# Three 256-column products in place of a 512- and a 256-column one, with the activations moved to another place in SBUF

## Chip, core and metric

The kernel runs on one core of a Trainium2 chip. The metric is the device time of one execution in microseconds, the median over runs. The profile is of one execution.

## What is computed

One decoder layer for 256 tokens of width 2048, in float32:

```python
h   = rmsnorm(x, attn_norm_g)
z   = h @ w_in                       # pool | q | k | v | indexer columns
x1  = x + concat(pool_mixer(...), dsa_attention(...)) @ w_out      # 2048 x 2048
up  = rmsnorm(x1, ffn_norm_g) @ w_up                               # 2048 x 11264
c   = conv_b + sum(conv_w[j] * shifted(up, j) for j in range(3))
gate, val = split(c, 2)
out = x1 + (silu(gate) * val) @ w_down                             # 5632 x 2048
```

## The kernel before

Every float32 operand of a large product is split into a high and a low half of type float32r, and a product is made of three terms: high x high, high x low and low x high. The activations stand as pairs (high, low) of 256 tokens each in three tiles: `xhl` (16 feature tiles; normed input first, then, overwritten, the input of the FFN), `yhl` (16, the input of w_out) and `ghl` (44, the input of w_down). The weights stream from HBM: `Unit.load` (L89) brings 1 MB into `raw` (two buffers), `Piece.split` (L103, L104) makes `whi` on ScalarE and `wlo` on VectorE (1024 columns each, four buffers of each), two pieces ahead of TensorE.

The order of the work is written out by hand: a list of pieces, each with its products, and `at(step, ...)`, which puts the other work between them. The stages run in this order: w_in in chunks (with the indexer, top-k, attention and pooling between them), w_out, w_up, w_down. For w_out, w_up and w_down the weight block of 128 x 128 is the stationary operand and the activations of 256 tokens move. One weight block (its high and its low half) with one feature tile is called a block here. There are 16 x 16 = 256 blocks in w_out, 88 x 16 = 1408 in w_up, and 16 x 44 = 704 in w_down.

A block is done by one of two helpers. `mm_feat` (L216, L217) loads the high weights once and streams both halves of the activations as one product of 512 columns, then loads the low weights and streams 256 columns. The products with the high and with the low half of the activations land in two halves of a PSUM bank, and whoever reads the result adds them (`up_out` L635 and L636, `down_out` L660 and L661). `mm_feat1` (L221 to L223) makes three products of 256 columns into one place, each with a weight load of its own. w_up and the first 14 of 16 column tiles of w_down use `mm_feat` (1408 + 616 blocks); w_out, the last two column tiles of w_down (88 blocks), the pool chunks of w_in and the pool mixer use `mm_feat1`. The other chunks of w_in (`mm_tok`, L210 to L212) hold the activations and move the weights, in products of 320 to 512 columns.

Where the tiles lie follows from the order of allocation, with no care for it in the code: modulo 512 bytes the weights' halves begin at 0, and one weight block is 512 bytes long in a partition; `xhl` begins at 256, `yhl` at 128, `ghl` at 0. The high or low half of a feature tile is 1024 bytes long, so all of a tile's halves begin at the same place modulo 512.

Of the kernel before, what the change touches and what calls it, by code (L numbers as in the profile page):

```python
# [8 lines left out]
F32 = mybir.dt.float32  # L9
F32R = mybir.dt.float32r  # L10
BF16 = mybir.dt.bfloat16
AF = mybir.ActivationFunctionType
ALU = mybir.AluOpType
AX = mybir.AxisListType

P = 128
S = 256
D = 2048
KT = D // P
IH = 16  # L20
DFF = 5632
NF = DFF // P
# [7 lines left out]
C_AG, C_FG, C_PS, C_QG, C_KG, C_IC, C_CW, C_CB = 0, 16, 32, 40, 41, 42, 58, 58 + 3 * 2 * NF  # L30
# [9 lines left out]
WARM = 8  # L40


@with_exitstack
def hybrid_kernel(ctx, tc, xT, par, wIa, wIb, wIc, wI2, wA, wU, wP, wO, wUp, wDn, out):
    nc = tc.nc
    PS = bass.MemoryType.PSUM

    cp = ctx.enter_context(tc.tile_pool(name="cp", bufs=1))
# [3 lines left out]

    pr = cp.tile([P, C_N], F32, name="pr")
    xf = cp.tile([P, KT, S], F32, name="xf")
    xhl = cp.tile([P, KT, 2, S], F32R, name="xhl")
    ga = cp.tile([P, KT], F32, name="ga")


# [32 lines left out]
    class Piece:  # L91


        def __init__(self, unit, a, b, mm):
            self.unit, self.a, self.b, self.mm = unit, a, b, mm
# [18 lines left out]
        sides.setdefault(step, []).append(lambda: f(*a))  # L114


    def split_x(k, src, gains, on_act):
        g = gains[:, k:k + 1]
        if on_act:
            nc.scalar.activation(xhl[:, k, 0], src, AF.Copy, scale=g)  # L120
        else:
            nc.vector.tensor_scalar(xhl[:, k, 0], src, g, None, op0=ALU.mult)
        nc.vector.scalar_tensor_tensor(xhl[:, k, 1], src, g, xhl[:, k, 0].bitcast(F32),  # L123
                                       op0=ALU.mult, op1=ALU.subtract)

    zp = ctx.enter_context(ExitStack())
    zc = zp.enter_context(tc.tile_pool(name="zc", bufs=1))
# [42 lines left out]
    r1, r2 = TokenNorm("r1"), TokenNorm("r2")  # L170
# [42 lines left out]

    def mm_feat(o, wh, wl, rhs, first, last):

        nc.tensor.matmul(o, wh, rhs.rearrange("p a t -> p (a t)"), start=first, stop=False)  # L216
        nc.tensor.matmul(o[:, 0:S], wl, rhs[:, 0], start=False, stop=last)  # L217

    def mm_feat1(o, wh, wl, rhs, first, last):

        nc.tensor.matmul(o[:, 0:S], wh, rhs[:, 0], start=first, stop=False)  # L221
        nc.tensor.matmul(o[:, 0:S], wh, rhs[:, 1], start=False, stop=False)  # L222
        nc.tensor.matmul(o[:, 0:S], wl, rhs[:, 0], start=False, stop=last)  # L223
# [13 lines left out]
    def pool_chunk(n):  # L237
        acc = Acc()
        for j in range(2):
            u = Unit(wU[2 * n + j], D)  # L240
            for h in range(2):
                def mm(p, j=j, h=h):
                    pt = acc.get()
                    for i in range(8):
                        k = 8 * h + i
                        mm_feat1(pt[:, j], *p.get(i * P, P), xhl[:, k], k == 0, k == KT - 1)
                pieces.append(Piece(u, h * 1024, (h + 1) * 1024, mm))
        return acc

    ia, za, ua, first = [], {}, [], {}  # L250
# [17 lines left out]
    for name in ORDER:  # L268
# [9 lines left out]
        else:  # L278
            c = ("k0", "k1", "q0", "q1", "v0", "v1").index(name)
            za[name] = tok_chunk([wA[c, q] for q in range(4)], 512)  # L280


    yhl = zc.tile([P, KT, 2, S], F32R, name="yhl")
    oa = [Acc() for g in range(8)]
    O0 = len(pieces)
    late = []
# [1 line left out]
    def mm_o(jp, j, ks, p, base):  # L288
        pt = oa[jp].get()
        for k in ks:  # L290
            mm_feat1(pt[:, j], *p.get((k - base) * P, P), yhl[:, k], k == 0, k == KT - 1)

    for jp in range(8):
        us = [Unit(wO[2 * jp + j], D) for j in range(2)]
        seq = [(j, h) for j in range(2) for h in range(2)]
        if jp == 0:
            seq = [(0, 0), (1, 0), (0, 1), (1, 1)]
        for j, h in seq:
            def mm(p, jp=jp, j=j, h=h):
                if jp == 0 and h == 1:  # L300
                    mm_o(jp, j, range(8, 14), p, 8)
                    late.append((jp, j, range(14, 16), p, 8))
                    if j == 1:
                        for a in late:
                            mm_o(*a)
                else:
                    mm_o(jp, j, range(8 * h, 8 * h + 8), p, 8 * h)
            pieces.append(Piece(us[j], h * 1024, (h + 1) * 1024, mm))
# [3 lines left out]
    for f in range(NF):  # L312
        us = [Unit(wUp[2 * f + j], D) for j in range(2)]
        seq = [(j, h) for j in range(2) for h in range(2)]
        if f == 0:
            seq = [(0, 0), (1, 0), (0, 1), (1, 1)]
        for j, h in seq:
            def mm(p, f=f, j=j, h=h):
                pt = ga_[f].get()
                for i in range(8):  # L320
                    k = 8 * h + i
                    mm_feat(pt[:, j], *p.get(i * P, P), xhl[:, k], k == 0, k == KT - 1)
            pieces.append(Piece(us[j], h * 1024, (h + 1) * 1024, mm))

    da = [Acc() for g in range(7)] + [Acc(single=True) for g in range(2)]
    D0 = len(pieces)
    ghl = None
    for i in range(16 * NF // 8):
        if i % 2 == 0:
            u = Unit(wDn[i // 2], 2048)  # L330

        def mm(p, i=i):
            for n in range(8):
                t, k = divmod(8 * i + n, NF)
                if t < 14:
                    mm_feat(da[t // 2].get()[:, t % 2], *p.get(n * P, P), ghl[:, k], k == 0, k == NF - 1)
                else:
                    mm_feat1(da[t - 7].get(), *p.get(n * P, P), ghl[:, k], k == 0, k == NF - 1)
        o = (i % 2) * 1024
        pieces.append(Piece(u, o, o + 1024, mm))  # L340

# [193 lines left out]
    pw_ = {}  # L535
# [49 lines left out]
    def pool_mix(n):  # L585
        g = GROUPS[n]
        hi, lo = pwt[n]
        for j in range(2):
            pt = ps_s.tile([P, 512], F32, name="pm", tag="ss")
            for k in range(2):  # L590
                c = slice(k * S + j * P, k * S + j * P + P)
                mm_feat1(pt, hi[:, c], lo[:, c], pw_[n][:, k], k == 0, k == 1)
            sc = pr[:, C_PS + 2 * g + j:C_PS + 2 * g + j + 1]
            y = yhl[:, 4 + 2 * n + 4 * (n == 3) + j]
            nc.scalar.activation(y[:, 0], pt[:, 0:S], AF.Copy, scale=sc)
            nc.vector.scalar_tensor_tensor(y[:, 1], pt[:, 0:S], sc, y[:, 0].bitcast(F32),
                                           op0=ALU.mult, op1=ALU.subtract)
# [4 lines left out]
    def x1_out(jp):  # L602
        pt = oa[jp].get()
        x1 = xf[:, 2 * jp:2 * jp + 2]
        nc.vector.tensor_tensor(x1, pt[:, :, 0:S], x1, op=ALU.add)
        for j in range(2):
            split_x(2 * jp + j, x1[:, j], pr[:, C_FG:C_FG + KT], True)
        if jp == 0:
            nc.scalar.activation(sq1, x1, AF.Square)
        else:  # L610
            t = zc.tile([P, 2, S], F32, name="xt", tag="t2", bufs=5)
            nc.scalar.activation(t, x1, AF.Square)
            nc.vector.tensor_tensor(sq1, sq1, t, op=ALU.add)
# [5 lines left out]
    fw = {}  # L619

    def ffn_open():
        nonlocal ghl
        zp.close()
        fp = ctx.enter_context(tc.tile_pool(name="fp", bufs=1))
        ghl = fp.tile([P, NF, 2, S], F32R, name="ghl")
        fw["up"] = [fp.tile([P, 2, S + 2], F32, name=f"up{i}") for i in range(2)]
        for u in fw["up"]:
            nc.gpsimd.memset(u[:, :, 0:2], 0.0)
        fw["fp"] = fp

    def up_out(f):
        fp = fw["fp"]
        pt = ga_[f].get()
        t = fp.tile([P, 2, S], F32, name="ft", tag="ft", bufs=2)
        nc.scalar.activation(t, pt[:, :, S:2 * S], AF.Copy)  # L635
        nc.vector.tensor_tensor(t, pt[:, :, 0:S], t, op=ALU.add)  # L636
        nc.vector.tensor_tensor(fw["up"][f % 2][:, :, 2:], t, r2.b2(), op=ALU.mult)

    def up_conv(f):
        u = fw["up"][f % 2]  # L640
# [16 lines left out]
    def down_out(jp):  # L657
        pt = da[jp].get()
        t = fw["fp"].tile([P, 2, S], F32, name="ft", tag="ft", bufs=2)
        nc.scalar.activation(t, pt[:, :, S:2 * S], AF.Copy)  # L660
        nc.vector.tensor_tensor(t, pt[:, :, 0:S], t, op=ALU.add)  # L661
        nc.vector.tensor_tensor(t, t, xf[:, 2 * jp:2 * jp + 2], op=ALU.add)
        nc.scalar.dma_start(out[:, 2 * jp:2 * jp + 2], t)

    def down_out1(jp, j):
# [80 lines left out]
    def prep(n):  # L746
        if n < 15 and n % 2 == 1:
            for k in (n + 1, n + 2):
                split_x(k, xf[:, k], ga, True)
        if n < len(pieces):  # L750
            pieces[n].split(2 if n == 0 else 1)
        if n == 0:
            for k in range(2):
                split_x(k, xf[:, k], ga, False)
# [73 lines left out]
```

## Time and profile before

| | us |
|---|---|
| median of 3 runs (lowest, highest) | 1098.84 (1098.68, 1098.87) |
| the profiled execution: its own time | 1098.5 |
| the profiled execution: span from first to last instruction | 1096.8 |
| TensorE busy in the span | 1090.8 |
| VectorE busy | 729.8 |
| ScalarE busy | 569.7 |

Some 1.7 us of the profiled execution lie outside its span. A product's recorded time contains its way through the array, so that consecutive products overlap in the records: what a product costs in a stream is the distance from its start to the next one's start, not its recorded time.

### The profile page before, as it was taken

How to read it: one execution, taken by the hardware profiler on the slowest of the kernel's cores; microseconds unless marked ns; L12 is line 12 of the kernel's file. 1: busy time of each engine (PE TensorE's matmuls, PEld its weight loads, DVE VectorE, ACT ScalarE, POOL GpSimd, SP SyncE). 2: the span in 40 equal slices, each digit the busy share in tenths (PEclk: the TensorE clock that was granted, in tenths of full speed). 3: DMA queues.
4: the chain of work that ended last, by engine and by line, in shares of the span. 5: the costliest groups of instructions: out<-in, count | busy, mean ns of one | idle time of the engine just before them, and what ended most of it. 6: DMA issues, size and time to landing. Idle time of an engine off the chain costs nothing.

```text
span 1096.8 us, 16441 instructions
## 1 busy us (share of the span) xinstructions
PE 1090.8 (99%) x6620; PEld 973.5 (89%) x6620; DVE 729.8 (67%) x1037; ACT 569.7 (52%) x796; POOL 13.8 (1%) x25
## 2 busy tenths in 40 slices
PE   9999999999999999999999999999999999999998
PEld 7988889889999888888888888888888888888898
DVE  7667857665565687777777777777787544444442
ACT  7555456654444555555555555555555443333441
POOL 0001000000000000000000000000000000000000
PEclk9999999999999999999999999999999999999999
DMA  8554564444555555555555555555555556555552
GB/s 289 169 188 148 178 231 156 164 163 154 171 180 189 192 192 192 189 184 192 186 189 183 191 191 192 188 192 192 192 192 192 193 201 201 197 195 198 195 197 74
DMA packets 31755, 204.30 MB, mean 186 GB/s; under 512 B 3648, under 2 KB 4288, under 8 KB 8640
## 3 DMA queue, kind: packets, MB, share of 16 engines
q1 hardware_dynamic: 30240, 201.16, 53.7%
q10 hardware_dynamic: 1440, 2.11, 0.5%
q8 instruction: 52, 0.85, 0.3%
q14 instruction: 23, 0.19, 0.0%
HBM read 201.15 MB, written 2.10 MB: 185 GB/s over the span
## 4 chain that ended last, share of the span: by engine, by line
PE 99%; DMA 1%; SPq 0%; ACT 0%; DVE 0%; issue 0%; ACTq 0%
PE mm L216 43%; PE mm L217 21%; PE mm L210 5%; PE mm L212 5%; PE mm L211 5%; PE mm L221 5%; PE mm L222 5%; PE mm L223 5%; PE sp L403 1%; DMA xf<-in_xT_dram 1%; PE sp L489 0%; PE tp L477 0%; PE op L529 0%; PE tp L517 0%; PE tp L393 0%; PE pm L221 0%
## 5 line engine op out<-in xcount | busy, mean ns | idle before, releaser
L104 DVE TENSOR_TENSOR wlo<-raw,whi 128x1024 fp32r<-128x1024 f32 (+4 forms) x385 | 462.6, 1203 | 296.2 <-ACT whi L103 294.9
L103 ACT ACTIVATE whi<-raw 128x1024 fp32r<-128x1024 f32 (+4 forms) x385 | 399.9, 1041 | 429.4 <-PE mm L216 262.4
L216 PE MATMUL mm<-xhl,whi 128*128 128x512 f32 x1408 | 488.4, 394 | 0.0
L217 PE MATMUL mm<-xhl,wlo 128*128 128x256 f32 x1408 | 390.1, 277 | 0.0
L216 PEld LDWEIGHTS mm<-xhl,whi 128*128 128x128 f32 x1408 | 264.0, 187 | 61.0
L217 PEld LDWEIGHTS mm<-xhl,wlo 128*128 128x128 f32 x1408 | 264.4, 188 | 0.0
L216 PE MATMUL mm<-ghl,whi 128*128 128x512 f32 x616 | 213.6, 394 | 0.0
L217 PE MATMUL mm<-ghl,wlo 128*128 128x256 f32 x616 | 170.6, 277 | 0.0
L216 PEld LDWEIGHTS mm<-ghl,whi 128*128 128x128 f32 x616 | 115.5, 188 | 26.8
L217 PEld LDWEIGHTS mm<-ghl,wlo 128*128 128x128 f32 x616 | 115.7, 188 | 0.0
L210 PE MATMUL mm<-whi,xhl 128*128 128x512 f32 (+3 forms) x288 | 108.3, 376 | 1.1 <-ACT xhl L120 0.5
L212 PE MATMUL mm<-whi,xhl 128*128 128x512 f32 (+3 forms) x288 | 106.8, 371 | 0.0
L211 PE MATMUL mm<-wlo,xhl 128*128 128x512 f32 (+3 forms) x288 | 106.6, 370 | 0.2 <-DVE wlo L104 0.2
L221 PE MATMUL mm<-yhl,whi 128*128 128x256 f32 x256 | 72.2, 282 | 0.0
L223 PE MATMUL mm<-yhl,wlo 128*128 128x256 f32 x256 | 72.1, 281 | 0.0
L222 PE MATMUL mm<-yhl,whi 128*128 128x256 f32 x256 | 72.1, 281 | 0.0
L210 PEld LDWEIGHTS mm<-whi,xhl 128*128 128x128 f32 x288 | 54.1, 188 | 9.0 <-issue 0.9
L212 PEld LDWEIGHTS mm<-whi,xhl 128*128 128x128 f32 x288 | 54.1, 188 | 8.3 <-DVE xhl L123 0.5
L211 PEld LDWEIGHTS mm<-wlo,xhl 128*128 128x128 f32 x288 | 54.1, 188 | 7.3 <-DVE wlo L104 0.4
L654 ACT ACTIVATE ghl<-fc 128x256 fp32r<-128x256 f32 x44 | 18.4, 417 | 57.8 <-DVE fc L653 57.8
L221 PEld LDWEIGHTS mm<-yhl,whi 128*128 128x128 f32 x256 | 48.2, 188 | 0.0
L222 PEld LDWEIGHTS mm<-yhl,whi 128*128 128x128 f32 x256 | 48.2, 188 | 0.0
(156 smaller groups left out, 955.6 us busy)
## 6 DMA issues: line engine op xcount, KB each, us to landing
raw<-in_wUp_dram SPq DMA_DIRECT2D x88, 1024.0 KB, 4.8
raw<-in_wDn_dram SPq DMA_DIRECT2D x44, 1024.0 KB, 4.8
raw<-in_wA_dram SPq DMA_DIRECT2D x24, 1024.0 KB, 4.8
raw<-in_wO_dram SPq DMA_DIRECT2D x16, 1024.0 KB, 4.8
raw<-in_wU_dram SPq DMA_DIRECT2D x8, 1024.0 KB, 5.0
raw<-in_wI_dram SPq DMA_DIRECT2D x4, 640.0 KB, 4.0
raw<-in_wIb_dram SPq DMA_DIRECT2D x3, 784.0 KB, 4.5
xf<-in_xT_dram SPq DMA_DIRECT2D x8, 256.0 KB, 4.9
```

The source lines that it names most:

```text
L103: i1 = nc.scalar.activation(hi, raw, AF.Copy)
L104: i2 = nc.vector.tensor_tensor(self.lo[:, c:c + n], raw, hi.bitcast(F32), op=ALU.subtract)
L210: nc.tensor.matmul(o, xhl[:, k, 0, t], wh, start=(k == 0), stop=False)
L211: nc.tensor.matmul(o, xhl[:, k, 0, t], wl, start=False, stop=False)
L212: nc.tensor.matmul(o, xhl[:, k, 1, t], wh, start=False, stop=(k == KT - 1))
L216: nc.tensor.matmul(o, wh, rhs.rearrange("p a t -> p (a t)"), start=first, stop=False)
L217: nc.tensor.matmul(o[:, 0:S], wl, rhs[:, 0], start=False, stop=last)
L221: nc.tensor.matmul(o[:, 0:S], wh, rhs[:, 0], start=first, stop=False)
L222: nc.tensor.matmul(o[:, 0:S], wh, rhs[:, 1], start=False, stop=False)
L223: nc.tensor.matmul(o[:, 0:S], wl, rhs[:, 0], start=False, stop=last)
L403: nc.tensor.matmul(sp[:, a:b], q, kiT[:, e, 0:b - a], start=(e == 0), stop=(e == 1))
L654: nc.scalar.activation(ghl[:, f, 0], c[:, 0], AF.Copy)
```

## The change

All three weight matrices now use three products of 256 columns per block; the name `mm_feat` goes to the former `mm_feat1`. The high and low terms then all lie in one half of the PSUM bank, and the copies and adds that joined the two halves are dropped from `up_out` and `down_out`. A new helper `placed` makes the activation tiles a little larger and begins the data some floats into them: `x2hl` (the FFN's input, in the memory of `xhl`) 112 floats = 448 bytes, `yhl` 16 floats = 64 bytes, `ghl` 48 floats = 192 bytes. Modulo 512 bytes each then begins at 192, and the weights' halves still at 0. `xhl` itself, for w_in, stays where it was.

```diff
+PLACE = {"x": 0, "x2": 112, "y": 16, "g": 48}
+def placed(pool, n, name, o, of=None):
+    m = n * 2 * S
+    t = of[0] if of else pool.tile([P, m + (128 if name == "xhl" else o)], F32R, name=name)
+    return t, t[:, o:o + m].rearrange("p (k a t) -> p k a t", k=n, a=2)
...
-    xhl = cp.tile([P, KT, 2, S], F32R, name="xhl")
+    xhl = placed(cp, KT, "xhl", PLACE["x"])
+    x2hl = placed(cp, KT, "xhl", PLACE["x2"], xhl)
+    xhl, x2hl = xhl[1], x2hl[1]
...
     def mm_feat(o, wh, wl, rhs, first, last):
-        nc.tensor.matmul(o, wh, rhs.rearrange("p a t -> p (a t)"), start=first, stop=False)
-        nc.tensor.matmul(o[:, 0:S], wl, rhs[:, 0], start=False, stop=last)
-
-    def mm_feat1(o, wh, wl, rhs, first, last):
         nc.tensor.matmul(o[:, 0:S], wh, rhs[:, 0], start=first, stop=False)
         nc.tensor.matmul(o[:, 0:S], wh, rhs[:, 1], start=False, stop=False)
         nc.tensor.matmul(o[:, 0:S], wl, rhs[:, 0], start=False, stop=last)
...
-    yhl = zc.tile([P, KT, 2, S], F32R, name="yhl")
+    yhl = placed(zc, KT, "yhl", PLACE["y"])[1]
...
-                    mm_feat(pt[:, j], *p.get(i * P, P), xhl[:, k], k == 0, k == KT - 1)
+                    mm_feat(pt[:, j], *p.get(i * P, P), x2hl[:, k], k == 0, k == KT - 1)
...
-            split_x(2 * jp + j, x1[:, j], pr[:, C_FG:C_FG + KT], True)
+            split_x(2 * jp + j, x1[:, j], pr[:, C_FG:C_FG + KT], True, x2hl)
...
-        ghl = fp.tile([P, NF, 2, S], F32R, name="ghl")
+        ghl = placed(fp, NF, "ghl", PLACE["g"])[1]
...
     def up_out(f):
-        fp = fw["fp"]
         pt = ga_[f].get()
-        t = fp.tile([P, 2, S], F32, name="ft", tag="ft", bufs=2)
-        nc.scalar.activation(t, pt[:, :, S:2 * S], AF.Copy)
-        nc.vector.tensor_tensor(t, pt[:, :, 0:S], t, op=ALU.add)
-        nc.vector.tensor_tensor(fw["up"][f % 2][:, :, 2:], t, r2.b2(), op=ALU.mult)
+        nc.vector.tensor_tensor(fw["up"][f % 2][:, :, 2:], pt[:, :, 0:S], r2.b2(), op=ALU.mult)
...
     def down_out(jp):
         pt = da[jp].get()
         t = fw["fp"].tile([P, 2, S], F32, name="ft", tag="ft", bufs=2)
-        nc.scalar.activation(t, pt[:, :, S:2 * S], AF.Copy)
-        nc.vector.tensor_tensor(t, pt[:, :, 0:S], t, op=ALU.add)
-        nc.vector.tensor_tensor(t, t, xf[:, 2 * jp:2 * jp + 2], op=ALU.add)
+        nc.vector.tensor_tensor(t, pt[:, :, 0:S], xf[:, 2 * jp:2 * jp + 2], op=ALU.add)
         nc.scalar.dma_start(out[:, 2 * jp:2 * jp + 2], t)
```

## Rows read from the trace of the kernel before

**Rows 1.** The page: busy time of the engines, and granted clock by slice.

```profile
PE 1090.8 (99%) x6620; PEld 973.5 (89%) x6620; DVE 729.8 (67%) x1037; ACT 569.7 (52%) x796; POOL 13.8 (1%) x25
...
PEclk9999999999999999999999999999999999999999
```

**Rows 2.** The page: the chain that ended last, shares by engine.

```profile
PE 99%; DMA 1%; SPq 0%; ACT 0%; DVE 0%; issue 0%; ACTq 0%
```

**Rows 3.** Waits of TensorE, first of five: total us, times, longest.

```profile
PE pw L63 <- DVE warm L60: 1.3, 1, 1.3
...
```

**Rows 4.** Groups of TensorE's products, forms apart: busy us, mean ns.

```profile
L216 PE MATMUL mm<-xhl,whi 128*128 128x512 f32 x1408 | 488.4, 394 | 0.0
L217 PE MATMUL mm<-xhl,wlo 128*128 128x256 f32 x1408 | 390.1, 277 | 0.0
...
L221 PE MATMUL mm<-yhl,whi 128*128 128x256 f32 x256 | 72.2, 282 | 0.0
```

**Rows 5.** Line L216 in w_up, then w_down: ns min/median/max, first to last start.

```profile
L216 PE MATMUL mm<-xhl,whi x578: 392/394/395, 399.8 to 599.9; 128*128 128x512 f32 x193
...
L216 PE MATMUL mm<-ghl,whi x578: 392/394/395, 849.8 to 1049.8; 128*128 128x512 f32 x193
```

**Rows 6.** Line L221 in w_out, then at the end of w_down.

```profile
L221 PE MATMUL mm<-yhl,whi x197: 279/281/285, 280.0 to 349.8; 128*128 128x256 f32 x197
...
L221 PE MATMUL mm<-ghl,whi x68: 283/283/283, 1068.8 to 1092.9; 128*128 128x256 f32 x68
```

**Rows 7.** Timeline of TensorE, a pool chunk of w_in: start us, us.

```profile
119.73 0.28 PE L223 MATMUL mm<-xhl,wlo 128*128 128x256 f32 x1
...
122.97 0.28 PE L223 MATMUL mm<-xhl,wlo 128*128 128x256 f32 x1
```

**Rows 8.** Timeline of TensorE, 512-column products of w_in.

```profile
99.70 0.39 PE L210 MATMUL mm<-whi,xhl 128*128 128x512 f32 x1
...
102.42 0.39 PE L210 MATMUL mm<-whi,xhl 128*128 128x512 f32 x1
```

**Rows 9.** Timeline of TensorE, 384-column products of w_in.

```profile
20.50 0.33 PE L210 MATMUL mm<-whi,xhl 128*128 128x384 f32 x1
...
21.89 0.33 PE L212 MATMUL mm<-whi,xhl 128*128 128x384 f32 x1
```

**Rows 10.** Timeline of TensorE, twelve 400-column products of w_in.

```profile
22.06 0.34 PE L210 MATMUL mm<-whi,xhl 128*128 128x400 f32 x1
...
23.14 0.34 PE L210 MATMUL mm<-whi,xhl 128*128 128x400 f32 x1
...
24.23 0.34 PE L210 MATMUL mm<-whi,xhl 128*128 128x384 f32 x1
```

**Rows 11.** The tile ghl on TensorE: ns min/median/max, first to last start.

```profile
L216 PE MATMUL mm<-ghl,whi x616: 392/394/395, 848.1 to 1061.3; 128*128 128x512 f32 x154
L217 PE MATMUL mm<-ghl,wlo x616: 274/277/280, 848.3 to 1061.5; 128*128 128x256 f32 x154
L221 PE MATMUL mm<-ghl,whi x88: 280/283/283, 1061.6 to 1092.9; 128*128 128x256 f32 x88
```

**Rows 12.** Groups of weight loads, forms apart: busy us, mean ns.

```profile
L223 PEld LDWEIGHTS mm<-yhl,wlo 128*128 128x128 f32 x256 | 48.2, 188 | 0.0
...
L223 PEld LDWEIGHTS mm<-ghl,wlo 128*128 128x128 f32 x88 | 16.9, 192 | 0.0
```

**Rows 13.** The chain in order of time, four transposes: start us, us.

```profile
51.76 0.43 PE tp L393 x4
```

**Rows 14.** The tile ft: ns min/median/max, first to last start.

```profile
L635 ACT ACTIVATE ft<-mm x44: 576/577/592, 371.9 to 849.2; 128x512 f32<-128x512 f32 x44
L636 DVE TENSOR_TENSOR ft<-mm,ft x44: 683/684/686, 372.9 to 850.4; 128x512 f32<-128x512 f32 x44
```

**Rows 15.** Windows, w_up: us, then busy us (count) of PE, PEld, DVE, ACT, POOL; clock, DMA.

```profile
380.00:740.00 360.00, 360.00 (x2079) 314.83 (x2078) 275.23 (x388) 205.26 (x292) 0.00 (x0) 1.00 0.56 190
```

**Rows 16.** The page: DMA issues of w_up, KB each, us to landing.

```profile
raw<-in_wUp_dram SPq DMA_DIRECT2D x88, 1024.0 KB, 4.8
```

More of the change, by code (lines that the diff above doesn't have):

```diff
@@ L114, in at, with split_x @@
         sides.setdefault(step, []).append(lambda: f(*a))
-    def split_x(k, src, gains, on_act):
+    def split_x(k, src, gains, on_act, xhl=xhl):
         g = gains[:, k:k + 1]
@@ L245, in mm @@
                         k = 8 * h + i
-                        mm_feat1(pt[:, j], *p.get(i * P, P), xhl[:, k], k == 0, k == KT - 1)
+                        mm_feat(pt[:, j], *p.get(i * P, P), xhl[:, k], k == 0, k == KT - 1)
                 pieces.append(Piece(u, h * 1024, (h + 1) * 1024, mm))
@@ L290, in mm_o @@
         for k in ks:
-            mm_feat1(pt[:, j], *p.get((k - base) * P, P), yhl[:, k], k == 0, k == KT - 1)
+            mm_feat(pt[:, j], *p.get((k - base) * P, P), yhl[:, k], k == 0, k == KT - 1)
     for jp in range(8):
@@ L337, in mm @@
                 else:
-                    mm_feat1(da[t - 7].get(), *p.get(n * P, P), ghl[:, k], k == 0, k == NF - 1)
+                    mm_feat(da[t - 7].get(), *p.get(n * P, P), ghl[:, k], k == 0, k == NF - 1)
         o = (i % 2) * 1024
@@ L591, in pool_mix @@
                 c = slice(k * S + j * P, k * S + j * P + P)
-                mm_feat1(pt, hi[:, c], lo[:, c], pw_[n][:, k], k == 0, k == 1)
+                mm_feat(pt, hi[:, c], lo[:, c], pw_[n][:, k], k == 0, k == 1)
             sc = pr[:, C_PS + 2 * g + j:C_PS + 2 * g + j + 1]
```

## The prediction, made before the changed kernel ran

> **What bounds the kernel now.** I read the page first. TensorE is busy for 99% of the span, at a granted clock of 1.0 in every slice, which is the 2.4 GHz level [rows 1]. The chain that ended last is TensorE for 99% [rows 2], and TensorE waited for another engine only five times, all at the start, the longest for 1.3 us [rows 3]. So the time is the sum of distances from the start of one product to the start of the next. The recorded durations overlap and are not these distances, so I took starts, a first and a last one with the products between them.
>
> A block of w_up (512 + 256 columns): 577 blocks from 399.8 to 599.9, 346.8 ns each; of w_down, 577 in 200.0 us, 346.6 ns [rows 5]. A block of three 256s: in w_out 196 blocks from 280.0 to 349.8, 356.1 ns, or 118.7 a product; at the end of w_down 67 blocks in 24.1 us, 359.7 ns, or 119.9 [rows 6]; in a pool chunk 27 products in 3.24 us, 120.0 each [rows 7].
>
> What does a column cost? Twelve products of 512 columns take 2.72 us, 226.7 ns each [rows 8]; eight of 384 take 1.39 us, 173.8 [rows 9]. The difference of 128 columns is 52.9 ns, or 0.41 ns a column, one column per cycle at 2.4 GHz. 256 columns are then 106.7 ns, and everything above is an extra: about 13.3 ns per product in each of these rows, whatever its length. The block of 512 + 256 pays two extras (346.7 − 320 = 26.7), the block of three 256s pays three (40 at the end of w_down). Each product comes with a weight load of its own, so the extra may belong to the load.
>
> **What the change does to this.** In w_up (1408 blocks) and w_down (616) a 512 + 256 becomes three 256s: the same columns, one product and one weight load more. In w_out (256) and in the last 88 blocks of w_down the shape stays, and only the place of the activations moves: from 128 (w_out) and 0 (w_down) to 192 modulo 512. For w_up it moves from 256 to 192. With p the distance of two 256-column products at the new place, and durations from above:
>
> w_up 1408 × (3p − 346.8) + w_down 616 × (3p − 346.6) + w_out 256 × (3p − 356.1) + end of w_down 88 × (3p − 359.7).
>
> One ns of p is 3 × 2368 = 7.1 us. The sum is zero at p = 116.1. Everything hangs on p, and no row shows a 256-column product at 192.
>
> *The bound above.* If place makes no difference, p is 118.7 to 120. At 120.0 the sum is 18.6 + 8.3 + 1.0 + 0.0 = +27.9 us.
>
> *The bound below.* If the extra vanishes, p = 106.7: −37.6 − 16.3 − 9.2 − 3.5 = −66.6 us. Issuing does not forbid it: four transposes with a load each take 0.43 us, 108 ns each [rows 13].
>
> *Does place matter at all?* It does, a little, in three rows. First, the same three products cost 118.7 with activations at 128 and 119.9 at 0, and at 128 their durations scatter over 279 to 285 ns where at 0 they are 283 each time [rows 6]. Second, the weight load beside them is recorded with 188 ns at 128 and 192 at 0 [rows 12]. Third, of the 400-column products of w_in, six that move weights from 0 take 1.08 us and the next six, whose weights begin 1600 bytes on (64 modulo 512), take 1.09 us, with the same held activations at 256 [rows 10]. That is 180.0 against 181.7: there the odd place is worse. A constant exchange of weights would not know addresses; a product's stream and the load of the next weights getting in each other's way would. A block of weights is 512 bytes and is read while 1024 bytes of activations go by, both streams running on modulo 512 from product to product, so where they meet depends on the distance between the places, and at one distance they may pass without meeting.
>
> *The value I take.* In each stream the distance is the recorded duration less about 162.5 ns (283 and 119.9, 281 and 118.7 [rows 6]; medians 394 + 277 against 346.7 [rows 4, 5, 11]). The shortest 256-column duration in the long stages is 274 ns, right after a 512 [rows 11]: a distance of about 112. It is the least held product that a row shows, 9 ns under the 283 of the same tile, and it lies in the middle between 106.7 and the 118.7 of the nearest place. I take p = 112, as an estimate. Against it: the 512 before it pays more, since a pair's mean stays at 346.7. At 112 a block is 336.0: w_up −15.2, w_down −6.5, w_out −5.1, end of w_down −2.1, together −28.9 us.
>
> The Trainium skill ("TensorE: Matmul & The Clock Gate", "Back-to-back issue gap") gives N/2.4 + 2.5 ns for an isolated product, 109.2 for 256 columns; by that figure the sum would be −48.8 us, 1050. The rows with a load per product lie over it by 9 ns or more.
>
> **The rest of the change costs nothing.** The copy of 577 ns on ScalarE and the add of 684 ns on VectorE fall away 44 times in w_up [rows 14] and seven times in w_down. They run under TensorE, which waits for neither; VectorE is busy 275 of 360 us in w_up [rows 15], and 76% goes to about 73%. If that cover were gone, the add would be 44 × 0.68 = 30 us to win, but it is not on the chain. The moved tiles bring no instruction. The read of PSUM becomes shorter. Faster blocks ask for weights sooner: 16 blocks use 1 MB in 5.55 us now, 5.38 at p = 112 and 5.12 at 106.7; one MB lands 4.8 us after issue with two buffers in turn [rows 16]. That stays hidden.
>
> **The rivals.** (a) *Place does not help: slower.* Nothing but the third extra is left in 2024 blocks. For it: seven kinds of product at several places pay 12 to 15 ns each, and the one row with an odd multiple of 64 is the worse one. The nearest places, 128 and 256, give 118.7 and 120.0: 1117 and 1126 us; with the 1.7 ns of the 400s on top, 1138. It decides from p = 116.4 upward.
>
> The Trainium skill speaks for this rival: by "SBUF — State Buffer", "Who interferes with whom", the moving operand and the weight load have independent read ports and TensorE waits on nobody. By that rule place changes nothing, and three 256s cost 120. The spread of rows 6 and 12 with place is not what that rule leads one to expect, but it is small.
>
> (b) *The two streams pass each other completely: faster still*, p from 106.7 to 109: 1032 to 1048. For it: 108 ns transposes. Against it: no 256-column product in these stages comes near. (c) *The gain of w_out and the loss elsewhere cancel*: p between 115.8 and 116.4, no measurable change; a narrow gap that nothing aims at. (d) *TensorE begins to wait* for a split or for weights, a faster TensorE held at the 4.8 us per MB: p could not fall under some 100 then, below the bound already.
>
> **How the numbers follow.** The sum is made against the profiled execution, 1098.5 us, of which 1.7 lie outside the span; it is 0.3 under the median of 1098.84. 1098.5 − 28.9 = 1069.6, with 0.3 for the median 1070. Chances: forecast, p from 109 to 115.8 (1048 to 1097): 0.45; (b) 0.17; (c) 0.04; (a) 0.34; (d) is in none of these. Faster 0.62, same 0.04, slower 0.34, where "same" is 0.2%, 2.2 us, about what a measurement of this kernel can tell. I put the better part on faster because the trace shows an extra that knows addresses, and 192 is a distance that no stream of 256s has tried; it is not more than that, since all places seen lie within 2 ns. The range goes from 1036 (p = 107.2) to 1127 (p = 120): both signs hold much of the chance, and the likeliest case alone is 1048 to 1097.
>
> **What would show it.** Right: in w_up, w_down and w_out alike 577 blocks take some 194 us (336 ns each), recorded durations fall to about 274, the loads stay at 188, and w_out alone loses some 5 us with no change of shape. Wrong as in (a): durations stay at 279 to 285 and blocks at 356 to 360, w_up longer by 13 to 19 us. If w_out improves but w_up does not, the place acts only with its own tile. PE waits of more than 3 us in w_up would mean (d).

## The result, and the profile after

The changed kernel takes 1079.57 us (median of 4 runs, 1079.27 to 1079.84) against 1098.82 (4 runs): a ratio of 0.9825, 95% interval 0.9808 to 0.9842, or 19.2 us less. The profiled execution took 1079.61 us, its span 1077.9.

The page, busy time of the engines (compare [rows 1]) and the chain by engine (compare [rows 2]):

```profile
PE 1072.1 (99%) x8644; PEld 1042.4 (97%) x8644; DVE 697.0 (65%) x986; ACT 544.9 (51%) x745; POOL 13.8 (1%) x25
...
PE 99%; DMA 1%; SPq 0%; ACT 0%; DVE 0%; issue 0%; ACTq 0%
```

TensorE is the chain as before, with 2024 products and as many weight loads more, in less time. Line L231, the first of a block's three products, in w_out, w_up and w_down (durations min/median/max, first to last start; compare [rows 5, 6]):

```profile
L231 PE MATMUL mm<-yhl,whi x207: 276/276/276, 279.8 to 349.8; 128*128 128x256 f32 x104
...
L231 PE MATMUL mm<-xhl,whi x589: 276/276/276, 399.9 to 599.8; 128*128 128x256 f32 x197
...
L231 PE MATMUL mm<-ghl,whi x589: 276/276/276, 850.0 to 1050.0; 128*128 128x256 f32 x197
```

588 blocks of w_up in 199.9 us are 340.0 ns each, 113.3 a product; w_down's are 340.1, and w_out's 206 in 70.0 us are 339.8. Every duration is 276, where three 256s took 279 to 285 at 128 and 283 at 0. By stages, from the blocks: w_up 1408 × (340.0 − 346.8) = −9.6; w_down 616 × (340.1 − 346.6) = −4.0; w_out 256 × (339.8 − 356.1) = −4.2; end of w_down 88 × (340.1 − 359.7) = −1.7. Together −19.5, against 19.2 less measured: whatever else changed is worth no more than some 0.3 us.

The weight loads and the window of w_up (compare [rows 12, 15]):

```profile
L233 PEld LDWEIGHTS mm<-xhl,wlo 128*128 128x128 f32 x1536 | 288.8, 188 | 0.0
L233 PEld LDWEIGHTS mm<-ghl,wlo 128*128 128x128 f32 x704 | 132.2, 188 | 0.0
```

```profile
380.00:740.00 360.00, 360.00 (x3179) 360.00 (x3179) 260.08 (x366) 193.25 (x265) 0.00 (x0) 1.00 0.55 194
```

Loads are 188 ns now in w_down too (192 before at its end). VectorE is busy for 260 of 360 us in place of 275: the dropped adds were cover, not path. The longest wait of TensorE and the landing of the weights (compare [rows 3, 16]):

```profile
PE pw L78 <- DVE warm L75: 1.3, 1, 1.3
...
raw<-in_wUp_dram SPq DMA_DIRECT2D x88, 1024.0 KB, 4.8
```

### The profile page after: what moved, and what is told of

It reads as the page before. It is cut to its first block, busy times and chain, and to the rows that moved or that the text cites. A ratio compares the mean times of both kernels' runs of the same rounds, so it can differ in the third digit from the quotient of the medians.

```text
span 1077.9 us, 20309 instructions
## 1 busy us (share of the span) xinstructions
PE 1072.1 (99%) x8644; PEld 1042.4 (97%) x8644; DVE 697.0 (65%) x986; ACT 544.9 (51%) x745; POOL 13.8 (1%) x25
## 4 chain that ended last, share of the span: by engine, by line
PE 99%; DMA 1%; SPq 0%; ACT 0%; DVE 0%; issue 0%; ACTq 0%
PE mm L233 26%; PE mm L231 26%; PE mm L232 26%; PE mm L225 6%; PE mm L227 5%; PE mm L226 5%; PE sp L413 1%; DMA xf<-in_xT_dram 1%; PE sp L499 0%; PE tp L487 0%; PE op L539 0%; PE tp L527 0%; PE tp L403 0%; PE pm L232 0%; PE pm L233 0%; PE pm L231 0%
## 5 line engine op out<-in xcount | busy, mean ns | idle before, releaser
L231 PE MATMUL mm<-xhl,whi 128*128 128x256 f32 x1536 | 426.1, 277 | 0.0
L233 PE MATMUL mm<-xhl,wlo 128*128 128x256 f32 x1536 | 424.9, 277 | 0.0
L232 PE MATMUL mm<-xhl,whi 128*128 128x256 f32 x1536 | 424.9, 277 | 0.0
L232 PEld LDWEIGHTS mm<-xhl,whi 128*128 128x128 f32 x1536 | 288.9, 188 | 0.2
L231 PEld LDWEIGHTS mm<-xhl,whi 128*128 128x128 f32 x1536 | 288.8, 188 | 0.2
L233 PEld LDWEIGHTS mm<-xhl,wlo 128*128 128x128 f32 x1536 | 288.8, 188 | 0.0
L231 PE MATMUL mm<-ghl,whi 128*128 128x256 f32 x704 | 194.3, 276 | 0.0
L232 PE MATMUL mm<-ghl,whi 128*128 128x256 f32 x704 | 194.3, 276 | 0.0
L233 PE MATMUL mm<-ghl,wlo 128*128 128x256 f32 x704 | 194.3, 276 | 0.0
L231 PEld LDWEIGHTS mm<-ghl,whi 128*128 128x128 f32 x704 | 132.2, 188 | 0.0
L232 PEld LDWEIGHTS mm<-ghl,whi 128*128 128x128 f32 x704 | 132.2, 188 | 0.0
L233 PEld LDWEIGHTS mm<-ghl,wlo 128*128 128x128 f32 x704 | 132.2, 188 | 0.0
L227 PE MATMUL mm<-whi,xhl 128*128 128x512 f32 (+3 forms) x288 | 106.7, 370 | 0.0
L231 PE MATMUL mm<-yhl,whi 128*128 128x256 f32 x256 | 70.8, 277 | 0.0
L232 PE MATMUL mm<-yhl,whi 128*128 128x256 f32 x256 | 70.7, 276 | 0.0
```

Source lines behind the costliest of these rows:

```text
L227: nc.tensor.matmul(o, xhl[:, k, 1, t], wh, start=False, stop=(k == KT - 1))
```

## Experiments

Theory 1 going in: the distance between where the activations and the weights begin, modulo 512 bytes, sets how much a weight load and the product beside it cost each other. The rivals: the shape of the products makes the gain, or the place of the activations by itself.

**Shape alone.**

```diff
-PLACE = {"x": 0, "x2": 112, "y": 16, "g": 48}
+PLACE = {"x": 0, "x2": 0, "y": 0, "g": 0}
```

> Three 256-column products per block everywhere, as in the changed kernel, but the activations back at their old places (256 in w_up, 128 in w_out, 0 in w_down). Theory 1, the place makes the gain: a product costs 120 ns in w_up and w_down and 118.7 in w_out, and the time is some 1126 us, slower than before by 27 to 28. Rival, the shape makes it (all three terms in one PSUM bank, no copies and adds): the products cost 113 ns without the place and the time is about 1080 us.

Measured: 1125.42 us (1125.27 to 1125.68), ratio to before 1.0241 (1.0226 to 1.0256). The same lines in this kernel:

```profile
L231 PE MATMUL mm<-xhl,whi x557: 283/283/284, 399.8 to 599.9; 128*128 128x256 f32 x186
...
L231 PE MATMUL mm<-ghl,whi x557: 283/283/284, 899.8 to 1100.0; 128*128 128x256 f32 x186
```

359.9 and 360.1 ns a block, 120 a product. The shape by itself costs 26 us; the place then gives back 46.

**Place alone.** The products of before, 512 + 256 columns, on tiles at 192. Both helpers are back as in the kernel before: w_out, the pool chunks and the end of w_down call `mm_feat1`. The copies and adds are back too; the diff does not show them.

```diff
     def mm_feat(o, wh, wl, rhs, first, last):
...
+        nc.tensor.matmul(o, wh, rhs.rearrange("p a t -> p (a t)"), start=first, stop=False)
+        nc.tensor.matmul(o[:, 0:S], wl, rhs[:, 0], start=False, stop=last)
+
+    def mm_feat1(o, wh, wl, rhs, first, last):
...
         nc.tensor.matmul(o[:, 0:S], wh, rhs[:, 0], start=first, stop=False)
```

> The activations at 192 as in the changed kernel, but w_up and w_down with 512 + 256 columns as before. If the place halves the extra of every weight load whatever the length of the product beside it, a block costs some 333 ns in place of 346.7 and the time is about 1066 us, better than the change. Rival: the streams pass each other only if they run in step, 512 bytes of weights to 1024 of activations, so that 512-column products keep their extra, a block keeps 346.7 ns, and only w_out (4 us) and the end of w_down (2 us) gain: about 1093 us.

Measured: 1107.84 us (1107.77 to 1108.12), ratio 1.0081 (1.0066 to 1.0096). Neither expectation holds: the block got dearer. Products of 512 columns in w_up, and three 256s (L236) at the end of w_down and in w_out:

```profile
L231 PE MATMUL mm<-xhl,whi x567: 397/397/398, 399.8 to 599.7; 128*128 128x512 f32 x189
...
L236 PE MATMUL mm<-ghl,whi x79: 281/281/282, 1075.0 to 1102.5; 128*128 128x256 f32 x79
...
L236 PE MATMUL mm<-yhl,whi x206: 276/276/277, 280.0 to 349.7; 128*128 128x256 f32 x103
```

566 blocks in 199.9 us are 353.2 ns, 6.5 more than at the old places. And the 88 blocks of three 256s, at the very distance at which the products of w_out last 276 ns in this kernel (340.0 ns a block), last 281, at 352.6 ns a block. The distance alone does not settle the cost; this was the first sign.

**Weights moved, activations of w_up left at 256.** 16 floats of padding ahead of the weights' buffers; w_out and w_down follow to 256.

```diff
-PLACE = {"x": 0, "x2": 112, "y": 16, "g": 48}
+PLACE = {"x": 0, "x2": 0, "y": 16, "g": 48}
...
     ga = cp.tile([P, KT], F32, name="ga")
+    cp.tile([P, 16], F32, name="gap")
```

> Three 256-column products; the activations of w_up stay at 256, where they were before, those of w_out and w_down begin at 256 too, and the weights' halves begin at 64 in place of 0: the distance is 192 again, but both lie elsewhere. Theory 1, the distance counts: 113.3 ns a product and about 1079.6 us. Rival, the place of the activations by itself counts: as with activations at 256 before, 120 ns a product and about 1126 us.

Measured: 1078.54 us (1078.41 to 1078.75), ratio 0.9815 (0.9798 to 0.9831). In w_up:

```profile
L232 PE MATMUL mm<-xhl,whi x589: 276/276/276, 400.0 to 600.0; 128*128 128x256 f32 x197
```

The activations lie where they did before and the product costs 113.4: it is the distance, not the place of either. (This kernel is 1 us under the changed one. Its pool chunks lie at distance 192 too, and their products take 116.1 ns in the mean, start to start, in place of 119.7.)

**A sweep of distances.** The weights of a piece begin some floats into their buffer; `wplace` gives 0, 16, ... 112 floats for 22 pieces of w_up each, and the steps named below for w_out and w_down.

```diff
     def split(self, parts=1):
...
+        self.off = wplace(pieces.index(self))
+        if self.off is not None:
+            m, o = 896, self.off
+            raw, hi = self.unit.raw[:, self.a:self.a + m], self.hi[:, o:o + m]
+            nc.scalar.activation(hi, raw, AF.Copy)
+            nc.vector.tensor_tensor(self.lo[:, o:o + m], raw, hi.bitcast(F32), op=ALU.subtract)
+            return
...
     def get(self, o, w):
+        if self.off is not None:
+            o = self.off + min(o, 768)
```

> Activations at 192, three 256-column products; the weights of w_up begin at 0, 64, ... 448 in eight stretches of 176 blocks each, those of w_out at 0, 64, 128, 192 in four, those of w_down at 0, 16, 32, 48, 496, 480, 464, 8 in eight. Every eighth block of a piece uses the weights of the seventh again, so this kernel leaves out an eighth of the products' terms. Theory 1 (only the distance counts, modulo 512): 113.3 ns a product at weights 0 (distance 192), 118.7 at weights 64 (distance 128), 120 at 192 and 448 (distances 0 and 256); the other four distances are unknown, 107 to 122. Rival (the place of the activations counts): 113.3 in all stretches. A step of 16 bytes near 192 should change little if the unit is 64 bytes, and by a part of the 6.5 ns if the streams meet at a finer grain.

Measured (one run, 1113.69 us; only its stretches are compared): w_up began with durations of 276 ns at distance 192 as expected; with the weights moved on, the other seven stretches had medians of 279 to 283 (at 448, for one, 141 blocks in 49.8 us, 353.2 ns each; at 0, 139 in 50.1, 360.4). But when w_down came back to distance 192, it did not come back to 276. Line L251, the first product of a block, at 448 in w_up and at 192 in w_down:

```profile
L251 PE MATMUL mm<-xhl,whi x142: 281/281/282, 610.0 to 659.8; 128*128 128x256 f32 x142
...
L251 PE MATMUL mm<-ghl,whi x71: 281/281/282, 860.0 to 884.8; 128*128 128x256 f32 x71
```

70 blocks in 24.8 us are 354.3 ns. Nothing odd stands before them but products at distance 256. So there are two steady speeds at one distance. The changed kernel's own trace has both: behind the column sums of the second norm (`pc`, products of one column) w_up has durations of 281 until the row products (`pb`, L178, products of 128 columns), and of 276 ever after.

```profile
L231 PE MATMUL mm<-xhl,whi x5: 281/281/281, 365.0 to 366.4; 128*128 128x256 f32 x5
```

That made theory 2: at this distance the stream has two steady states, and whatever interrupts it decides in which it goes on.

**One disturbance.** The changed kernel, with two one-column products into a tile that nobody reads.

```diff
+    def kick_cols():
+        pk = ps_s.tile([P, 512], F32, name="pk", tag="ss")
+        for th in range(2):
+            nc.tensor.matmul(pk[:, th:th + 1], sq1[:, 0, th * P:(th + 1) * P], ones[:, 0:1], start=True, stop=True)
...
+    at(G0 + 88, kick_cols)
```

> The changed kernel with one thing added: in the middle of w_up two products of one column into a PSUM tile that nobody reads, of the shape and operands that the column sums of the second norm have at the start of w_up. Theory 2: at distance 192 a stream of 256-column products has two steady states, 113.3 and 117.7 ns a product, and such a disturbance decides in which it goes on; after the column sums of the changed kernel it went on at 118, after the row products at 113. Then the 704 blocks of w_up behind the added products and the 704 of w_down run at 117.7, and the time is 1079.6 + 1408 x 3 x 4.4 ns = about 1098 us, for two products of a tenth of a microsecond. Rival: the distance alone sets the cost, and the kernel comes out at 1080 us.

Measured: 1098.95 us (10 runs, 1098.29 to 1099.59), ratio to before 1.0002 (0.9992 to 1.0012): the whole gain of the change is gone. Line L231 ahead of the disturbance and behind it, and the disturbance itself:

```profile
L231 PE MATMUL mm<-xhl,whi x559: 275/276/277, 400.0 to 589.7; 128*128 128x256 f32 x187
...
L231 PE MATMUL mm<-xhl,whi x595: 280/281/282, 620.0 to 829.9; 128*128 128x256 f32 x199
...
L231 PE MATMUL mm<-ghl,whi x595: 281/281/282, 869.8 to 1079.7; 128*128 128x256 f32 x199
...
L741 PE MATMUL pk<-ones,sq x4: 164/250/250, 595.2 to 595.4; 128*128 128x1 f32 x4
```

340.0 ns a block ahead of 595 us, 353.4 behind it, to the end of w_down 497 us later: 1408 × 13.4 = 18.9 us. The weight loads tell the two states apart as well. The load for the second product of a block (L232), in the changed kernel and then in this one behind the disturbance:

```profile
L232 PEld LDWEIGHTS mm<-xhl,whi x589: 187/188/188, 399.9 to 599.8; 128*128 128x128 f32 x197
...
L232 PEld LDWEIGHTS mm<-xhl,whi x595: 191/192/193, 620.0 to 829.9; 128*128 128x128 f32 x199
```

**And back.** The same, and two pieces later two plain float32 products of 128 columns.

```diff
+    def kick_rows():
+        pk = ps_s.tile([P, 512], F32, name="pk", tag="ss")
+        for th in range(2):
+            nc.tensor.matmul(pk[:, th * P:(th + 1) * P], ones, r2.dg[:, th], start=True, stop=True)
+
+    at(G0 + 88, kick_cols)
+    at(G0 + 90, kick_rows)
```

> The changed kernel with the two one-column products in the middle of w_up, as in the run that cost 19 us, and two pieces later two products of 128 columns in plain float32, the shape of the row products. Theory 2 (the last disturbance decides the state): only the 16 blocks between the two run at 117.7 ns a product, and the time is 1079.6 + 0.2 + some 0.7 us for the added products = about 1080.5 us. Rival (the one-column products do lasting harm, by their PSUM tile or by a delay that is never made up): about 1098 us as without the second disturbance.

Measured: 1080.89 us (1080.25 to 1083.18), ratio 0.9841 (0.9828 to 0.9855). Behind both:

```profile
L231 PE MATMUL mm<-xhl,whi x589: 276/276/277, 619.9 to 819.9; 128*128 128x256 f32 x197
```

The second disturbance undoes the first. The loss is a state, not a delay.

**The sweep with disturbances**, row products at the start of each stretch and column sums in its middle, for three 256s and for 512 + 256:

```diff
+    for n in range(1, 8):
+        at(G0 + 22 * n, kick_rows)
+    for n in range(8):
+        at(G0 + 22 * n + 11, kick_cols)
+        at(D0 + 11 * n, kick_rows)
+        at(D0 + 11 * n + 5, kick_cols)
```

> The sweep of weights' places with three 256-column products, with a disturbance at the start and in the middle of each stretch of w_up and w_down: row products (two of 128 columns in plain float32) at the start, column sums (two of one column) in the middle. As in the first sweep, every eighth block of a piece repeats the weights of the seventh, so an eighth of the terms is left out. Theory 2: at distance 192 the half behind the row products runs at 113.3 ns a product and the half behind the column sums at 117.7; the other odd multiples of 64 (64, 320, 448), which ran at 117.7 in the first sweep, have the same two states; 0 and 256 stay at 120 and 128 and 384 at 118.7 in both halves. Rival: the two states belong to distance 192 alone, the other distances are the same in both halves.

> The same sweep and disturbances with 512 + 256 columns in w_up and w_down (an eighth of the terms left out as there). At distance 192 without disturbance this block took 353.4 ns (235.1 + 118.3), at the places before, distances 256 and 0, 346.7. If the distance sets the extra as with 256 columns, the odd multiples of 64 give 353 and the even ones 347, in each half alike. Rival: a 512-column block also has two states, and one half of the stretch at distance 192 falls to 333 ns or less.

Measured (one run each, 1127.93 and 1119.63 us; only their stretches are compared) in w_up, ns a block, each from the first and last start of line L251 within the half stretch (76 to 80 blocks, good to some 1.3 ns; 46 and 51 in the first half at 192, which had the kernel's own row products):

| distance | three 256s, behind row products | behind column sums | 512 + 256, behind row products | behind column sums |
|---|---|---|---|---|
| 192 | 340.0 | 353.8 | 353.3 | 353.2 |
| 128 | 359.7 | 355.1 | 350.6 | 351.4 |
| 64 | 353.9 | 353.2 | 353.9 | 354.5 |
| 0 | 360.3 | 361.0 | 346.2 | 346.7 |
| 448 | 339.0 | 353.2 | 352.6 | 354.1 |
| 384 | 360.3 | 357.0 | 351.9 | 350.7 |
| 320 | 353.9 | 353.9 | 352.6 | 353.2 |
| 256 | 360.0 | 360.0 | 346.6 | 346.6 |

Three 256s at distances 448, 320 and 128, each behind row products and then behind column sums:

```profile
L251 PE MATMUL mm<-xhl,whi x78: 276/276/277, 613.8 to 639.9; 128*128 128x256 f32 x78
L251 PE MATMUL mm<-xhl,whi x80: 280/281/282, 643.8 to 671.7; 128*128 128x256 f32 x80
...
L251 PE MATMUL mm<-xhl,whi x77: 279/279/280, 739.9 to 766.8; 128*128 128x256 f32 x77
L251 PE MATMUL mm<-xhl,whi x77: 278/279/280, 771.8 to 798.7; 128*128 128x256 f32 x77
...
L251 PE MATMUL mm<-xhl,whi x78: 282/285/288, 423.0 to 450.7; 128*128 128x256 f32 x78
L251 PE MATMUL mm<-xhl,whi x79: 279/281/285, 455.1 to 482.8; 128*128 128x256 f32 x79
```

512 + 256 at distance 192 and at 0:

```profile
L251 PE MATMUL mm<-xhl,whi x78: 389/397/398, 391.7 to 418.9; 128*128 128x512 f32 x78
...
L251 PE MATMUL mm<-xhl,whi x79: 392/392/395, 549.0 to 576.0; 128*128 128x512 f32 x79
```

Theory 2 holds at 192 and at 448, and the cost repeats every 256 bytes. Three expectations missed: 64 and 320 have one state only; 128 and 384, expected to have one, have two that differ by some 4 ns a block, and there the row products leave the dearer one; and 512 + 256 takes 351 at 128 and 384, where 347 was expected. With 512 + 256 there is no good state at 192; the old places, 0 and 256, were that block's best of the eight. In w_down, 144 to 240 in steps of 16 and 184, no other distance came to 340. At 208 the row products again leave the dearer state, first row, and the column sums the cheaper, second row:

```profile
L251 PE MATMUL mm<-ghl,whi x31: 281/291/291, 995.8 to 1006.9; 128*128 128x256 f32 x31
...
L251 PE MATMUL mm<-ghl,whi x43: 280/280/281, 1009.9 to 1024.8; 128*128 128x256 f32 x43
```

30 blocks in 11.1 us are 370.0 ns, the dearest of all; 42 in 14.9 us are 354.8. So which odd product sets the good state depends on the distance.

**The pool chunks as well.**

```diff
-PLACE = {"x": 0, "x2": 112, "y": 16, "g": 48}
+PLACE = {"x": 48, "x2": 112, "y": 16, "g": 48}
```

> The changed kernel with the input of w_in moved as well, from 256 to 448 modulo 512: the 128 blocks of the pool chunks then lie at distance 448, which in the sweep had the same two states as 192. Theory 2: those blocks run at 113.3 or 117.7 ns a product in place of 120, according to what stands before them, 0.9 to 2.6 us less; the token chunks, which hold the activations and move the weights, get another distance too, and where the weights lay at 64 and the activations at 256 their 512-column products took 229 to 230 ns in place of 227, 1 to 2 us more. Together 1077.5 to 1080 us. Rival: distances 192 and 448 differ for this tile, and the pool blocks stay at 120: 1080 to 1082 us.

Measured: 1078.99 us (1078.51 to 1079.37), ratio to before 0.9821 (0.9807 to 0.9834), not to be told from the changed kernel. The first pool chunk and a piece of the last one:

```profile
L231 PE MATMUL mm<-xhl,whi x27: 281/281/281, 112.5 to 121.7; 128*128 128x256 f32 x27
...
L231 PE MATMUL mm<-xhl,whi x14: 276/276/285, 252.5 to 256.9; 128*128 128x256 f32 x14
```

The first chunk keeps durations of 281 and the last one, from its second block on, has 276, though both stand behind 512-column products; why they differ was not found. The 512-column products of the token chunks pay for the gain:

```profile
99.27 0.39 PE L227 MATMUL mm<-whi,xhl 128*128 128x512 f32 x1
...
102.48 0.39 PE L226 MATMUL mm<-wlo,xhl 128*128 128x512 f32 x1
```

14 products in 3.21 us, 229.3 each where [rows 8] give 226.7. Other stretches of w_in move less: start to start, the 536 of the 576 that follow one another take 229.5 ns in the mean against 228.3 in the changed kernel, some 0.7 us in all, and the 384 products of the pool chunks 115.9 against 119.7, some 1.5 us less.

## Why the prediction was right, and where it was off

- *The bound.* TensorE's starts set the time, and one ns of p is 7.1 us: held. The stage sum with the measured distances gives 19.5 us less, against 19.2 measured.
- *p = 112.* The term that was mis-sized: measured 113.3, so 1.33 × 7.1 = 9.5 us of the 28.9 did not come. 1079.6 lies within the forecast's own range, 1048 to 1097.
- *Why 112.* The number came out near for a reason that does not hold. The 274 ns after a 512 was read as a product that is held less; the place-alone run shows that a 512 + 256 block gains nothing at 192 and loses 6.5 ns. The remark against it, that the pair's mean stays put, was the better reading. So the number was in good part luck. What is shown is that half of the extra of 13.3 ns goes (6.7 is left), not that the streams pass each other.
- *The distance counts.* Shown by moving the weights and leaving the activations of w_up. That the distance alone decides, which the argument took for granted, is wrong: the same distance costs 113.3 or 117.7 according to the last interruption. The sign hung on that too, and the prediction did not know of it: with all blocks at 117.8 ns a product its own sum, zero at 116.1, gives 1.7 × 7.1 = 12 us more than before (an estimate; no run had all of them there). That the row products come last ahead of nearly all of w_up was luck.
- *The rest costs nothing.* TensorE waits four times, at most 1.3 us, VectorE went to 72%, 1 MB of weights still lands in 4.8 us: held.
- *Rival (a), place does not help.* Its price was right to a microsecond, 1126 against 1125.42 with the places undone; it was not the case. The rule of the Trainium skill that speaks for it ("SBUF — State Buffer", "Who interferes with whom": independent read ports, TensorE waits on nobody) is not borne out by these runs: with the same products, addresses alone are worth 46 us.
- *Rival (b), p of 109 or less:* no distance or state of the sweeps came near; 113.3 is the least mean.

The bound below, 106.7, deserves a second look. The 108 ns of the transposes speak less for it than the prediction took them to: they are products of 128 columns, half as many (first row below). In the run with one disturbance the four loads of the one-column products, and the load behind them, start 110 ns apart in the mean (second and third row):

```profile
51.59 0.60 PE L393 MATMUL tp<-ident,qst 128*128 128x128 f32 x4
...
595.07 0.52 PEld L741 LDWEIGHTS pk<-ones,sq 128*128 128x128 f32 x4
595.51 0.19 PEld L231 LDWEIGHTS mm<-xhl,whi 128*128 128x128 f32 x1
```

So with half the columns, or hardly any, a product with a load of its own still took 108 to 110 ns, more than the 106.7 of 256 columns, and 113.3 is only 3 to 5 ns above these rows. That the load sets such a floor under p is argued, not shown.

What stays open: what in the hardware the two states are. That product and load hinder each other is argued from the dependence on their distance, not shown, and why, at 192 and 448, row products set the good state and column sums the bad one was not found. Nor was it tested what in them does it: the two differ in columns and in operands.

## What to carry to other kernels

Where every product has a weight load of its own, compare distances from start to start with the columns alone; if an extra remains, try the distance between the moving and the held operand in 64-byte steps before changing shapes, and judge shape and place together: each of the two alone made this kernel slower. Look at the durations along the whole stage, not at their mean: here two odd products set the speed of a stream for hundreds of microseconds, and two cheap products of another shape set it back.

## What was not expected of the hardware

- Two steady speeds of one instruction stream at distances 192 and 448: 113.3 and 117.7 ns a product, each kept for as long as nothing came between; the dearer one, once for 497 us, to the end of the kernel.
- Two products of one column, some 0.4 us of TensorE, cost 19 us of a 1080 us kernel.
- Over the eight distances in steps of 64, the cost of three 256s repeats every 256 bytes, and two 256-column products do not follow the 512-column one: the best distance for the one (192: 340 ns a block) is among the worst for the other (353).
